# Squaring block 2's rows ahead of block 1's, its diagonal two stages earlier, and a fourth temporary buffer in phase three

## The chip, the cores and the metric

The kernel runs on one core of a Trainium2 chip. Its time is the device time of one execution in microseconds (us), the median of several; a profile is one execution recorded by the hardware profiler, with times counted from its first instruction. The engines are TensorE (PE, with its weight loads PEld), VectorE (DVE), ScalarE (ACT) and GpSimd (POOL). SyncE (SP) issues most loads, POOL issues the stores of the first part; each queue issues in order, and an instruction that waits holds back everything behind it on its queue.

## The reference

One step of a decoder layer on 4096 prompt tokens and 64 sample tokens (8 sequences of 8), with a model width of 1024, in float32:

```
def _layer(x, ...):
    h = _rmsnorm(x, g_pre)            # x * rsqrt(mean(x*x) + eps) * g_pre, row by row
    z = h @ w_in                      # 1024 -> 2816 columns
    ... gated short convolution, sliding-window attention, attention to 256 memory tokens ...
    y = concatenate([out_a, out_b, out_c]) @ w_out
    return x + _rmsnorm(y, g_post), ...
```

The change touches the first two lines only: how the factor rsqrt(mean(x*x) + eps) of each token, its row factor, comes to the place where the product h @ w_in is formed. It also touches the temporary tiles in which parts of z are kept until they are stored. What is computed stays the same.

## The kernel before

**Blocks, phases, steps.** The 4160 tokens are cut into 8 blocks (b = 0 to 7) of 520. A block's x stands transposed, in four operands B11, B21, B12, B22: the first digit is the half of the 1024 inputs, the second the half of the 520 tokens (128 partitions x 4 x 260 each). The 22 column tiles of w_in are taken in three phases (`PHASES`, L44) of 8, 8 and 6 tiles. "Phase three" is index 2. Within a phase each block is seven products of sums of weight quarters with sums of operands (`PRODUCTS`, L41; T1 to T4 are differences of the B operands, formed by `t_sum`), so that seven steps do the work of eight. Each product is three matmuls with operands split into a high and a low part (`split`, L357: `hi` by ScalarE, `lo` by VectorE, L360 and L361), all on L370.

**The plain blocks.** Blocks 0 and 1 of the first phase (`PLAIN_BLOCKS = 2`) run as eight plain products instead, the stages (b, s) with s = 0 to 7 of `PLAIN` (L578). TensorE can start on them before any row factor is known: the factors are multiplied into the results z afterwards (`z_rows`, L621). From block 2 on the operands are scaled before the product: `gain` (L326, ScalarE, by g_pre) and `scale` (L335, VectorE, by the row factors).

**Row factors.** For each block five groups of 104 tokens are loaded in natural layout (`row_load`, L255, on SP's queue), squared and summed by ScalarE (`row_step`, L269, L278), and turned into factors by POOL (L284, L285). j counts the groups, five to a block. From there two ways lead to a tile that has the 520 factors in every partition:
- For blocks 0 and 2 (`PLAIN_BLOCKS` is 2) `rows_diag` (L294) has VectorE write the factors on five diagonals, and `rows_product` (L302) has TensorE multiply them by ones; ScalarE copies the result out of PSUM (L308). `rows_bank` (L299) takes the PSUM bank for it.
- For the other blocks POOL stores the 520 factors to memory (`rowd`, L290, an issue of its own for 2 KB with the elements apart), and SP loads them back, broadcast to all partitions (`rows_load`, L251, L253). The load is issued a number of stages after the store: `row_spreads[b] = 4` counts down once a stage in `row_queue` (L310). Block 0 is stored too, for the next phase.

**The order of the work.** In the plain blocks and all of the first phase the order on every engine's queue is that of the program, by hand (`manual_schedule`, L697). `plain_loads` (L660) gives the loads of a stage, x operands first and then `row_queue`; `plain_jobs` (L628) gives a list of jobs for each stage, and `plain_block` (L674) spreads that list over the four quarters of the stage's matmuls, in proportion. With s at 2, 3, 6, 7 the second and the fourth quarter are followed by copies of the accumulators out of PSUM (L688). A natural row tile j >= 14 is loaded a stage after a square has freed its place (`row_loads`).

In the kernel before, the squares of block 1 (j = 5 to 9) end in stage (0, 7), and its store of factors follows there; those of block 2 (j = 10 to 14) end in (1, 2). The diagonal of block 2 is written in (1, 4) and multiplied in (1, 5). Block 1's factors are loaded in (1, 3) and first used by `z_rows(1, 1)` in (1, 7). Block 2's operands are loaded in (1, 2) to (1, 5), in the order B11, B21, B12, B22. Their gains and scales are jobs of (1, 4) to (1, 7).

**Phase three.** Phases two and three are ordered by the program's own scheduler, but for single instructions that are kept in place. `temp` (L170) hands out the temporary tiles. In phase three there are two pools of three tiles, `t2a` and `t2b` (L118), taken in turn unless the caller names one; each call turns the turn. `finish_parts` (L401) takes two for a tile of z in block 0: `zh`, the high part (L411), from pool a for the first row of a pair and from b for the second, and `kl_`, the low part (L413), by the turn. Later blocks write the low part in place. Both parts are stored to memory by SP (`qd`, L168), and a tile can be taken again when its store has landed.

Of the kernel before, what the change touches and what calls it, by code (L numbers as in the profile page):

```python
# [12 lines left out]
ALU = mybir.AluOpType  # L13
# [7 lines left out]
NS = 64  # L21
# [23 lines left out]
PLAIN_BLOCKS = 2  # L45
# [7 lines left out]
def hybrid_layer(ctx: ExitStack, tc: tile.TileContext, a: dict):  # L53
    nc = tc.nc
    TE, V, S, G, DMA = nc.tensor, nc.vector, nc.scalar, nc.gpsimd, nc.sync
# [40 lines left out]
    own = ExitStack()  # L96
# [6 lines left out]
    def open_phase(ph):  # L103
        nonlocal tp, natp, pa2, pa1, wide
        wide = 0 if ph == 0 else 2

        if ph == 0:
            z = [z_pool(kept_z, f"z{n}") for n in range(4)]
            natp = own.enter_context(tc.tile_pool(name="nat", bufs=2))
            zp[2] = [*z, z_pool(own, "z4")]  # L110
            kept_z.z4 = zp[2][-1]
        elif ph == 1:
            zp[2].remove(kept_z.z4)
            zp[2][:0] = [z_pool(own, f"z{n}") for n in (5, 6, 7)]
# [129 lines left out]
    RG = 104  # L244
# [3 lines left out]

    row_loads, row_spreads = [], {}

    def rows_load(b, again=False):  # L251
        rows[b] = (temp(f"rb{b}")[:, : 2 * HW] if again else natp.tile([P, 2 * HW], F32, tag="rb", name=f"rb{b}"))
        DMA.dma_start(rows[b], rowd[b].partition_broadcast(P))  # L253

    def row_load(j):  # L255
        if j < 5 * NBLK:
            g = RG * j - NS
            if 2 <= j < 10 or 12 <= j < 14:
                t = (wa if j < 7 or j == 12 else wb).tile([P, 2, 512], F32, tag="w", name=f"nat{j}")
                t = nat[j] = t.rearrange("p a n -> p (a n)")  # L260
            else:
                t = nat[j] = natp.tile([P, D], F32, tag="nat", name=f"nat{j}")
            if g < 0:
                DMA.dma_start(t[:NS], a["x_s"])
                DMA.dma_start(t[NS:RG], a["x_p"][: RG - NS, :])
            else:
                DMA.dma_start(t[:RG], a["x_p"][g : g + RG, :])

    def row_step():  # L269

        j = sq[0]
        if j == 5 * NBLK:
            return
        b, i = divmod(j, 5)
        if i == 0:
            nat["r"] = tiny.tile([P, 8], F32, tag="r", name=f"r{b}", bufs=3)
        r, t = nat["r"], nat.pop(j)
        S.activation(t[:RG], t[:RG], AF.Square, accum_out=r[:RG, i : i + 1])  # L278
        if j in (10, 11) or j >= 14:
            row_loads.append(after_nat[0])  # L280
            after_nat[0] += 1
        sq[0] += 1
        if i == 4:
            G.tensor_scalar(r[:RG, 0:5], r[:RG, 0:5], 1.0 / D, EPS, op0=ALU.mult, op1=ALU.add)  # L284
            G.tensor_tensor(r[:RG, 0:5], r[:RG, 0:5], mhalf[:RG, 0:5], op=ALU.pow)  # L285
# [4 lines left out]
            G.dma_start(rowd[b].rearrange("(i p) -> p i", p=RG), r[:RG, 0:5])  # L290
            if b > 0:
                row_spreads[b] = 4

    def rows_diag():  # L294

        for i in range(5):
            V.tensor_scalar(diag[:RG, RG * i : RG * (i + 1)], ident[:RG, :RG], nat["factors"][:RG, i : i + 1], None, op0=ALU.mult)

    def rows_bank(b):  # L299
        rows[b] = accumulator(1, 2, f"rows_y{b}")[:, :, :HW]  # L300
# [327 lines left out]
    def plain_jobs(b, s):  # L628

        gains = lambda b, *os: [lambda o=o: x_gain(0, b, o) for o in os]  # L630
        scales = lambda b, *os: [lambda o=o: x_scale(0, b, o) for o in os]
        parts = lambda b, o: [lambda: x_split(b, o)]
        fill = lambda o: [lambda q=q: first_fill(o, q) for q in range(4)]
        sums = lambda q, k: [lambda: first_sums(q, k)]
        fills = lambda q, *os: [lambda o=o: first_fills(q, o) for o in os]
        done = lambda b, row: finish(0, b, zz[b], row)
        row = [row_step]
        return {
            (0, 0): lambda: [*fill("A11"), *parts(0, "B21")],
            (0, 1): lambda: fill("A22"),  # L640
            (0, 2): lambda: [*fill("A12"), *parts(0, "B12"), *row],
            (0, 3): lambda: [*sums(0, 0), *row, *sums(0, 1), *fills(0, "S2"), *row],
            (0, 4): lambda: [*parts(0, "B22"), *fills(0, "S3", "S1"), *row, *fills(0, "S4"), *row],
            (0, 5): lambda: [*sums(1, 0), *row, *sums(1, 1), *fills(1, "S2", "S3"), *row],
            (0, 6): lambda: [*parts(1, "B11"), *row, *fills(1, "S1", "S4"), *sums(3, 0), *row],
            (0, 7): lambda: [*row, *fills(3, "S2", "S3"), lambda: rows_diag()],
            (1, 0): lambda: [*parts(1, "B21"), *row, *row, lambda: rows_bank(0), lambda: rows_product(0), *z_rows(0, 1)],
            (1, 1): lambda: [*z_rows(0, 0), *done(0, 1), *row, *row],
            (1, 2): lambda: [*parts(1, "B12"), *done(0, 0), *fills(3, "S1"), *row],
            (1, 3): lambda: sums(2, 0),  # L650
            (1, 4): lambda: [*row, lambda: rows_diag(), lambda: rows_bank(2), *parts(1, "B22"), *gains(2, "B11"), *sums(2, 1),
                             *fills(2, "S2")],
            (1, 5): lambda: [lambda: rows_product(2), *fills(2, "S3"), *row, *fills(2, "S1"), *gains(2, "B21"), *fills(2, "S4"),
                             *row],
            (1, 6): lambda: [*scales(2, "B11"), *gains(2, "B12"), *scales(2, "B21", "B12"), *row],
            (1, 7): lambda: [lambda: h_split(0), *gains(2, "B22"), *scales(2, "B22"), lambda: t_sum(0, 2, "T1"), *row,
                             *z_rows(1, 1)],
        }[b, s]()
# [1597 lines left out]
```

## Time and profile before

| | |
|---|---|
| median of three runs | 1470.48 us (1470.12 to 1474.75) |
| the profiled execution's own time | 1470.74 us |
| its span, first to last instruction | 1469.0 us |
| granted TensorE clock, mean | 0.999 |
| busy: PE, DVE, ACT, POOL | 1453.3, 1235.0, 888.9, 431.9 us |
| the plain blocks, stage (0, 0) to (1, 7) | about 6 to 100 us |
| phase three | about 662 to 930 us |

A line of a timeline gives start and duration in us, the engine, the line of the kernel, the operation with the tile that it writes and those that it reads, the shape, how many instructions are merged, and in brackets how long the engine was idle before it and what ended that. `SPq` and `ACTq` are an engine's issuing side. Names of tiles stand without their numbers at the end, so `hi_1B` is any high part of block 1's B operands. A line of waits gives the waiting engine, tile and line, what it waited for, the total in us, how often, and the longest. Matmul durations are modelled and overlap; their starts tell more.

### The profile page before, as it was taken

How to read it: one execution, taken by the hardware profiler on the slowest of the kernel's cores; microseconds unless marked ns; L12 is line 12 of the kernel's file. 1: busy time of each engine (PE TensorE's matmuls, PEld its weight loads, DVE VectorE, ACT ScalarE, POOL GpSimd, SP SyncE). 2: the span in 40 equal slices, each digit the busy share in tenths (PEclk: the TensorE clock that was granted, in tenths of full speed). 3: DMA queues.
4: the chain of work that ended last, by engine and by line, in shares of the span. 5: the costliest groups of instructions: out<-in, count | busy, mean ns of one | idle time of the engine just before them, and what ended most of it. 6: DMA issues, size and time to landing. Idle time of an engine off the chain costs nothing.

```text
span 1469.0 us, 31997 instructions
## 1 busy us (share of the span) xinstructions
PE 1453.3 (99%) x11887; PEld 1342.3 (91%) x11887; DVE 1235.0 (84%) x1991; ACT 888.9 (61%) x2170; POOL 431.9 (29%) x544
## 2 busy tenths in 40 slices
PE   9999999999999999999999999999999999999997
PEld 9999999999999999999999999778888888888875
DVE  6779887899988888798677777899998999999975
ACT  6776565566532222244545444788888878888862
POOL 0222322312403474300021130234334333433452
PEclk9999999999999999999999999999999999999999
DMA  9999999887866676688897679997887788888876
GB/s 265 191 248 223 297 275 265 248 288 248 216 229 244 243 248 232 225 284 253 281 233 266 215 215 329 279 280 240 252 263 241 240 243 268 243 248 264 254 266 224
DMA packets 233744, 369.59 MB, mean 252 GB/s; under 512 B 38501, under 2 KB 144485, under 8 KB 233557
## 3 DMA queue, kind: packets, MB, share of 16 engines
q1 hardware_dynamic: 210549, 314.66, 69.4%
q0 software_dynamic: 22320, 51.84, 12.4%
q8 instruction: 94, 1.54, 0.5%
q10 hardware_dynamic: 720, 1.05, 0.2%
q14 instruction: 61, 0.50, 0.1%
HBM read 251.00 MB, written 117.46 MB: 251 GB/s over the span
## 4 chain that ended last, share of the span: by engine, by line
PE 89%; DVE 4%; DMA 3%; ACT 2%; issue 1%; POOL 0%; ACTq 0%; SPq 0%; DVEq 0%; POOLq 0%
PE c L370 54%; PE y_c L1701 20%; PE ws L1394 3%; PE wo L1508 2%; PE wo L1115 2%; PE xs L1441 2%; PE wo L1503 1%; PE wt L1461 1%; PE xt L1461 1%; PE mem_acc L797 1%; DMA md<-th 1%; DMA nat<-in_x_p 1%; DMA ws4A<-in_w_in 1%; PE y L2069 1%; DMA md<-cacc 0%
## 5 line engine op out<-in xcount | busy, mean ns | idle before, releaser
L377 DVE TENSOR_TENSOR z<-c,z 128x520 f32<-128x520 f32 (+1 forms) x308 | 193.8, 643 | 71.8 <-PE c L370 70.8
L1425 ACT ACTIVATE sm<-sm,wnm 128x129 f32<-128x129 f32 x240 | 93.5, 392 | 13.8 <-DVE wrd L1429 7.1
L1701 PE MATMUL y_c<-wob,rows 128*128 128x512 f32 x384 | 95.8, 396 | 0.4 <-ACT s L1739 0.4
L1701 PE MATMUL y_c<-woT,a 128*128 128x512 f32 x384 | 95.2, 395 | 0.0
L1701 PE MATMUL y_c<-woT,down 128*128 128x512 f32 (+1 forms) x396 | 95.2, 389 | 0.0
L1701 PEld LDWEIGHTS y_c<-wob,rows 128*128 128x128 f32 x384 | 70.6, 188 | 17.5 <-ACT wpt L1366 2.4
L1701 PEld LDWEIGHTS y_c<-woT,down 128*128 128x128 f32 x396 | 71.7, 188 | 15.8 <-DVE swnm L1996 0.4
L1701 PEld LDWEIGHTS y_c<-woT,a 128*128 128x128 f32 x384 | 70.6, 188 | 15.2
L1232 ACT ACTIVATE xp<-xs,xnm 128x256 f32<-128x256 f32 x128 | 59.9, 483 | 20.4 <-PE wo L1115 13.5
L918 POOL TENSOR_TENSOR os0T<-os0T,os1T 128x512 f32<-128x512 f32 x20 | 29.0, 1448 | 125.2 <-DMA os1T<-in_w_out 75.8
L411 ACT CAST zh<-z 128x520 fp32r<-128x520 f32 x56 | 33.3, 625 | 40.9 <-DVE z L377 32.9
L1394 PEld LDWEIGHTS ws<-ring,q 128*128 128x128 f32 (+1 forms) x480 | 48.6, 186 | 8.4 <-issue 1.2
L278 ACT ACTIVATE nat<-nat 104x1024 f32<-104x1024 f32 x40 | 42.3, 1057 | 23.0 <-DMA nat<-in_x_p 23.0
L1411 DVE COPY_PREDICATED sm<-wmask,ws 128x512 f32<-128x512 uint8 x60 | 43.7, 754 | 14.6 <-ACT sm L1405 14.6
L1455 ACT ACTIVATE xp<-xp,xrd 128x256 f32<-128x256 f32 x120 | 53.9, 503 | 2.1 <-DVE xrd L1238 1.1
L1394 PE MATMUL ws<-ring,q 128*128 128x256 f32 (+1 forms) x480 | 54.0, 294 | 1.1 <-issue 0.6
L1366 ACT COPY wpt<-wt 128x512 f32<-128x512 f32 x60 | 33.9, 593 | 27.4 <-PE wo L1508 27.4
L379 ACT COPY z<-c 128x520 f32<-128x520 f32 (+1 forms) x44 | 24.2, 553 | 43.0 <-PE c L370 40.0
L1701 PE MATMUL y_c<-woT,diag 128*128 128x512 f32 x192 | 48.8, 400 | 0.0
L1369 POOL TENSOR_SCALAR_AFFINE_SELECT wpt<-wpt 128x512 f32<-128x512 f32 x64 | 46.1, 740 | 7.0 <-ACT wpt L1368 6.9
L1641 POOL TENSOR_TENSOR yst<-yst,mhalf 128x1 f32<-128x1 f32 (+1 forms) x33 | 20.4, 617 | 93.7 <-DVE yst L1640 93.7
L166 POOL DMA_DIRECT2D md<-th x48 | 26.2, 547 | 67.6 <-DVE th L430 59.4
(1055 smaller groups left out, 5537.9 us busy)
## 6 DMA issues: line engine op xcount, KB each, us to landing
woT<-tdT SPq DMA_DIRECT2D x75, 512.0 KB
q<-qd SPq DMA_DIRECT2D x112, 192.0 KB
xr<-in_x_p SPq DMA_DIRECT2D x32, 512.0 KB
nat<-in_x_p SPq DMA_DIRECT2D x39, 416.0 KB
o_yp<-xr SPq DMA_DIRECT2D x31, 512.0 KB
md<-th POOLq DMA_DIRECT2D x48, 260.0 KB, 7.2
qd<-zh SPq DMA_DIRECT2D x48, 260.0 KB
qd<-z SPq DMA_DIRECT2D x42, 260.0 KB
```

Of the source, the lines that this page charges most:

```text
L278: S.activation(t[:RG], t[:RG], AF.Square, accum_out=r[:RG, i : i + 1])
L370: TE.matmul(bank[:, :HW], l, r, start=first and i == 0, stop=last and i == 3 * KH - 1)
L377: add = lambda dst, other: V.tensor_tensor(dst, c, other, op=ALU.add)
L411: S.copy(hi, z)
L1232: S.activation(p[:, i, :], s[:, i, :], AF.Exp, bias=nm[:, i : i + 1], scale=SCALE, accum_out=den[:, i : i + 1])
L1366: S.copy(p3.rearrange("p h (r q) -> p r h q", r=2), t)
L1369: select = lambda out, step, op, slope: lambda: G.affine_select(out, p3, pattern=[[0, 4], [step, P]], compare_op=op, fill=0.0, base=0, cha ...
L1394: TE.matmul(out(kvh, col, bank), q(kvh, col, bank)[r], k(kvh, part)[r], start=first, stop=True, skip_group_check=not first, **place)
L1411: V.copy_predicated(self.of[i].sms[kvh][:, :, :P].rearrange("p (h a) k -> p a h k", a=2), third["wmask"].unsqueeze(1).to_broadcast([P, 2, ...
L1425: S.activation(sm[:, hh, :], sm[:, hh, :], AF.Exp, bias=nm[:, hh : hh + 1], scale=SCALE, accum_out=den[:, hh : hh + 1])
L1455: S.mul(p[:, i, :], p[:, i, :], self.rds[h][:, i : i + 1])
L1701: TE.matmul(self.acc[bank], self.parts[name][:, l, j], wo[o][j][:, r, cs], start=new and j + i == 0, stop=j == 3 and i == 2, skip_group_ch ...
```

## The change

Three edits. First, rows are squared in another order: `row_block` exchanges blocks 1 and 2, so that j = 5 to 9 are block 2's groups and j = 10 to 14 block 1's. The loads (`row_load`), the accumulators and the factors follow. Block 1's factors are therefore stored in (1, 2) instead of (0, 7), and their load comes two counts after the store instead of four, in (1, 4). The factors of blocks 0 and 2 are kept apart by key. Second, block 2's diagonal is written at the end of (1, 2) instead of in (1, 4); its product stays in (1, 5). The job list of (1, 2) grows from seven to eight, that of (1, 4) shrinks by one, and the spread over the quarters follows. Third, pool `t2b` of phase three gets a fourth tile.

```
-            tp = [own.enter_context(tc.tile_pool(name=f"t2{n}", bufs=3)) for n in "ab"]
+            tp = [own.enter_context(tc.tile_pool(name=f"t2{n}", bufs=3 + (n == "b"))) for n in "ab"]
...
+    def row_block(n):
+        return {1: 2, 2: 1}.get(n, n)
...
-            g = RG * j - NS
+            g = RG * (5 * row_block(j // 5) + j % 5) - NS
...
-        b, i = divmod(j, 5)
+        b, i = row_block(j // 5), j % 5
...
             if b in (0, PLAIN_BLOCKS):
-                nat["factors"] = r
+                nat["factors", b] = r
             if b == PLAIN_BLOCKS:
                 return
             G.dma_start(rowd[b].rearrange("(i p) -> p i", p=RG), r[:RG, 0:5])
             if b > 0:
-                row_spreads[b] = 4
+                row_spreads[b] = 2 if b < PLAIN_BLOCKS else 4
...
-            (1, 2): lambda: [*parts(1, "B12"), *done(0, 0), *fills(3, "S1"), *row],
+            (1, 2): lambda: [*parts(1, "B12"), *done(0, 0), *fills(3, "S1"), *row, lambda: rows_diag(2)],
             (1, 3): lambda: sums(2, 0),
-            (1, 4): lambda: [*row, lambda: rows_diag(), lambda: rows_bank(2), *parts(1, "B22"), *gains(2, "B11"), *sums(2, 1),
+            (1, 4): lambda: [*row, lambda: rows_bank(2), *parts(1, "B22"), *gains(2, "B11"), *sums(2, 1),
                              *fills(2, "S2")],
```

`rows_diag` takes the block as its argument; the call for block 0 in (0, 7) is otherwise unchanged.

More of the change, by code (lines that the diff above doesn't have):

```diff
@@ L291, in row_step, with rows_diag @@
             if b > 0:
-                row_spreads[b] = 4
-    def rows_diag():
+                row_spreads[b] = 2 if b < PLAIN_BLOCKS else 4
+    def rows_diag(b):
         for i in range(5):
-            V.tensor_scalar(diag[:RG, RG * i : RG * (i + 1)], ident[:RG, :RG], nat["factors"][:RG, i : i + 1], None, op0=ALU.mult)
+            V.tensor_scalar(diag[:RG, RG * i : RG * (i + 1)], ident[:RG, :RG], nat["factors", b][:RG, i : i + 1], None, op0=ALU.mult)
     def rows_bank(b):
@@ L645, in plain_jobs @@
             (0, 6): lambda: [*parts(1, "B11"), *row, *fills(1, "S1", "S4"), *sums(3, 0), *row],
-            (0, 7): lambda: [*row, *fills(3, "S2", "S3"), lambda: rows_diag()],
+            (0, 7): lambda: [*row, *fills(3, "S2", "S3"), lambda: rows_diag(0)],
             (1, 0): lambda: [*parts(1, "B21"), *row, *row, lambda: rows_bank(0), lambda: rows_product(0), *z_rows(0, 1)],
             (1, 1): lambda: [*z_rows(0, 0), *done(0, 1), *row, *row],
-            (1, 2): lambda: [*parts(1, "B12"), *done(0, 0), *fills(3, "S1"), *row],
+            (1, 2): lambda: [*parts(1, "B12"), *done(0, 0), *fills(3, "S1"), *row, lambda: rows_diag(2)],
             (1, 3): lambda: sums(2, 0),
-            (1, 4): lambda: [*row, lambda: rows_diag(), lambda: rows_bank(2), *parts(1, "B22"), *gains(2, "B11"), *sums(2, 1),
+            (1, 4): lambda: [*row, lambda: rows_bank(2), *parts(1, "B22"), *gains(2, "B11"), *sums(2, 1),
                              *fills(2, "S2")],
```

## The prediction

> **What bounds the kernel now.** I read the page first, then the stretches by engine, then TensorE's waits, and last the timelines around the two waits that lie where the change works.
>
> ```profile
> PE 1453.3 (99%) x11887; PEld 1342.3 (91%) x11887; DVE 1235.0 (84%) x1991; ACT 888.9 (61%) x2170; POOL 431.9 (29%) x544
> ...
> 0.00:115.00 115.00, 113.18 (x914) 112.11 (x915) 83.37 (x134) 83.36 (x162) 21.95 (x38) 1.00 0.94 227
> 656.00:930.00 274.00, 272.75 (x2228) 266.08 (x2226) 204.61 (x330) 130.21 (x238) 31.31 (x47) 1.00 0.80 250
> ```
>
> The columns of a stretch are its length, the busy time of PE, PEld, DVE, ACT and POOL, the granted clock, the DMA share and GB/s. TensorE is busy 99% of the span, so an edit elsewhere is worth only what it takes from TensorE's waits, or adds to them. The plain blocks and the first steps after them (0 to 115 us) leave TensorE idle 115.00 - 113.18 = 1.8 us; phase three (656 to 930 us) leaves 1.25 us. That is the most the change can win in its two places: 3 us, or 0.2%. Its possible loss has no such cap.
>
> ```profile
> PE c L370 <- DVE lo_1B L361: 1.0, 1, 1.0
> PE c L370 <- DVE lo_2T L361: 0.2, 1, 0.2
> ...
> 111.74 0.28 PE L370 MATMUL c<-hi_2T,w_0S 128*128 128x260 f32 x1
> 112.21 0.39 PE L370 MATMUL c<-lo_2T,w_0S 128*128 128x260 f32 x1 [0.18 <-DVE lo_2T L361]
> ...
> 696.24 0.28 PE L370 MATMUL c<-hi_1B,w_2A 128*128 128x260 f32 x1
> 696.36 0.28 PE L370 MATMUL c<-hi_1B,w_0A 128*128 128x260 f32 x1
> 697.60 0.39 PE L370 MATMUL c<-lo_1B,w_0A 128*128 128x260 f32 x1 [0.96 <-DVE lo_1B L361]
> ```
>
> Two waits of TensorE on L370 matter. Matmuls start 0.12 us apart when nothing holds them (696.24 to 696.36), so the first wait costs 112.21 - 111.74 - 0.12 = 0.35 us and the second 697.60 - 696.36 - 0.12 = 1.12 us.
>
> **The fourth buffer of pool t2b.** In phase three `temp` takes pools a and b in turn. Counting its calls, b receives two weight tiles of the first step, then the three `kl_` tiles of block 0's first row, then the second row's zh, kl_, zh, kl_, zh, kl_. With three buffers the second row's first zh follows the first kl_ (9004), and its first kl_ (9072) follows the second (9021):
>
> ```profile
> 689.27 0.32 SPq L168 DMA_DIRECT2D qd<-kl__9004  x1
> 690.18 0.81 SPq L168 DMA_DIRECT2D qd<-kl__9021  x1
> 694.28 0.63 ACT L411 CAST zh<-z 128x520 fp32r<-128x520 f32 x1 [3.75 <-DMA qd<-kl__9004]
> 694.81 1.05 ACT L360 CAST hi_1B<-x_1B 128x1040 fp32r<-128x1040 f32 x1
> 695.69 0.70 DVE L413 TENSOR_TENSOR kl__9072<-z,zh 128x520 fp32r<-128x520 f32 x1 [2.85 <-DMA qd<-kl__9021]
> 696.31 1.24 DVE L361 TENSOR_TENSOR lo_1B<-x_1B,hi_1B 128x1040 fp32r<-128x1040 f32 x1
> ```
>
> With four, that zh follows a weight tile that is long used up, and 9072 follows 9004, whose store has landed by 694.28 instead of 695.69. So 9072 runs 1.41 us earlier, and lo_1B ends near 697.55 - 1.41 = 696.14, before TensorE asks for it at 696.36 + 0.12. The wait of 1.12 us goes; what is late next is the same pair of tiles one step on, with some 4 us of matmuls ahead of it. The edit adds no instruction. Value: -1.1 us, between -1.25 (all idle of that stretch) and 0 (the program orders phase three itself, and with another buffer it may put the 9072 subtraction or the zh cast elsewhere).
>
> **The diagonal, two stages up.** Five multiplications leave VectorE's queue in stage (1, 4) and enter at the end of (1, 2):
>
> ```profile
> 81.86 1.00 DVE L297 TENSOR_SCALAR mix_s<-ident,r 104x104 f32<-104x104 f32 x5
> 84.72 0.59 ACT L308 COPY rb<-rows_y 128x520 f32<-128x520 f32 x1 [1.20 <-PE rows_y L306]
> ```
>
> They end 1.9 us before ScalarE may read the product, and the product itself stays in (1, 5), behind a quarter of that stage's matmuls. ScalarE waits for TensorE there, and not for the diagonal. Value 0; if the cover were gone, 1.0 us.
>
> **The order of the squares.** Ten squares, ten loads of the same sizes, one store of row factors and one load of them trade places: the counts stay, so the order itself costs 0. What moves is the pair store and load of block 1's factors (`rowd[1]`). The store goes from the end of (0, 7) to the end of (1, 2), past the md, zd and qd stores on POOL; the load goes from (1, 3) to (1, 4) on SP, past the two loads of block 2's B12. Between them lie two stages instead of four. How long does such a store take?
>
> ```profile
> 54.23 0.99 POOL L290 DMA_DIRECT2D rowd<-r  x1 [0.31 <-POOL r L285]
> DMA to landing us min/median/max: 9.3/11.8/14.5
> L253 SPq EVENT_SEMAPHORE  x6: 17/17/17, 78.2 to 266.7; - x6
> 54.00:61.00 7.00, 7.00 (x57) 6.88 (x56) 5.55 (x13) 5.69 (x13) 0.99 (x1) 1.00 0.90 209
> 61.00:67.00 6.00, 6.00 (x53) 6.00 (x52) 4.41 (x6) 2.52 (x5) 2.23 (x4) 1.00 1.18 79
> 67.00:75.00 8.00, 8.00 (x69) 8.00 (x69) 3.14 (x7) 4.95 (x10) 1.08 (x2) 1.00 0.99 285
> ```
>
> The second line is the answer for the tile rowd: its stores take 9.3 to 14.5 us to land. The third shows that the load L253 carries a wait on SP. The stretches show what the store does beside that: some 7 us after its issue, all transfers together fall to 79 GB/s for 6 us. TensorE stays full in it.
>
> The Trainium skill, page "DMA: Bandwidth & Descriptors", section "Latency and other measured facts", gives a DMA a fixed cost of about 2 us. By that the store would be down before SP asks, and the sum would be that of the second rival below, 1469.6 us. The row of landing times disagrees by a factor of five. The same page's "Rules for kernel authors" tells us to issue a DMA early and to wait for it late, and the edit does the reverse.
>
> *When the store starts.* In (1, 2) the last square releases it:
>
> ```profile
> 68.29 1.06 ACT L278 ACTIVATE nat<-nat 104x1024 f32<-104x1024 f32 x1 [4.77 <-DMA nat<-in_x_p]
> 74.20 0.64 ACT L429 ACTIVATE th<-z 128x520 f32<-128x520 f32 x1 [1.61 <-DMA md<-th]
> 76.61 1.07 ACT L278 ACTIVATE nat<-nat 104x1024 f32<-104x1024 f32 x1
> 78.36 1.19 POOL L285 TENSOR_TENSOR r<-r,mhalf 104x5 f32<-104x5 f32 x1
> ```
>
> At the old times it would start at 78.36 + 1.19 + 0.31 = 79.9 us. But the slow stretch at 61 to 67 us belongs to the store that is no longer there, and the square at 68.29 and the tanh at 74.20 wait for transfers out of it. Up to 4.77 us come back, so the start lies between 75.1 and 79.9. I take 76.0, nearer the early end, since both waits have the same cause.
>
> *When it lands.* Between 9.3 and 14.5 us later. Here SP, once held, adds no traffic of its own, so I take 10.5, between the shortest and the median 11.8: 86.5 us.
>
> *What stands behind it.* SP reaches the load of `rowd[1]` well before that and stops. Queued behind it are the two loads of block 2's B22 and the natural rows of the 17th square, which now leave late. ScalarE waits for those rows already:
>
> ```profile
> 78.23 0.34 SPq L253 DMA_DIRECT2D rb<-rowd  x1
> 82.19 10.73 SPq L267 DMA_DIRECT2D nat<-in_x_p  x3
> 91.43 1.06 ACT L278 ACTIVATE nat<-nat 104x1024 f32<-104x1024 f32 x1 [1.90 <-DMA nat<-in_x_p]
> 97.62 0.60 ACT L688 COPY z<-c 128x520 f32<-128x520 f32 x1 [0.26 <-PE c L370]
> 98.11 1.72 ACT L328 ACTIVATE place<-place,gpre 128x260 f32<-128x260 f32 x4
> 110.92 1.23 DVE L361 TENSOR_TENSOR lo_2T<-x_2T,hi_2T 128x1040 fp32r<-128x1040 f32 x1
> 99.90:112.10 12.20, 12.12 (x102) 11.91 (x100) 12.20 (x13) 8.24 (x15) 5.82 (x8) 1.00 0.86 200
> nat<-in_x_p SPq DMA_DIRECT2D x3, 416.0 KB
> rb<-rowd SPq DMA_DIRECT2D x1, 260.0 KB
> qd<-zh POOLq DMA_DIRECT2D x1, 260.0 KB, 3.5
> 83.00:91.00 8.00, 8.00 (x66) 7.88 (x66) 6.10 (x11) 5.33 (x12) 0.00 (x0) 1.00 0.95 235
> ```
>
> From 91.43 on ScalarE works in order, with one pause of 0.26 us, up to the gains of B22 at 98.11, and from their end VectorE is busy for all of 12.20 us until lo_2T, the tile of the first wait above. So whatever the 17th rows are late beyond 0.26 us reaches TensorE in full. Once the hold ends, 260 KB of factors, 520 KB of B22 (128 x 1040 x 4 bytes) and 416 KB of rows have to come: 1196 KB, which at 235 GB/s is 5.2 us. The lead is some 2 us: a lone 260 KB transfer lands in 3.5 us, of which about 1.1 us is its bytes. So 7 us, from 5.5 (the queue empty) to 9.2 (82.19 to 91.43, a full queue). The rows come at 86.5 + 7.0 = 93.5, which is 2.1 us after 91.43, and 1.8 us beyond the pause. Value +1.8 us. Bounds: 75.1 + 9.3 + 5.5 = 89.9 gives 0; 79.9 + 14.5 + 7.0 = 101.4 gives +9.7.
>
> **Sum.** -1.1 + 0 + 0 + 1.8 = +0.7 us. The profiled execution took 1470.74 us (span 1469.0, the rest around it); the median of the runs shown is 1470.48, 0.26 below. On the execution's own time: 1471.4 us.
>
> **The rivals.**
> - *The hold runs long (slower than before).* Nothing comes back from the old slow stretch, because the tanh at 74.20 has other stores ahead of it, and the store starts at 79.9 us and takes the median 11.8: it lands at 91.7, the rows come at 98.7, 7.0 us late beyond the pause. 1470.74 + 7.0 - 1.1 = 1476.6 us. It decides the sign from a landing after about 85.8 us, and passes 0.3% (4.4 us) from 90.2 us on. For it: every row of landing times is over 9 us. Against it: the 4.77 us wait has no other owner in the trace. Chance 0.16.
> - *The hold costs nothing.* The store starts early and lands before 84.7 us, or the loads behind it come in well under 7 us since the queue is empty. Then only the buffer counts: 1470.74 - 1.1 = 1469.6 us. For it: the shortest landing is 9.3 us, and SP, held, adds no traffic. Against it: it needs the early end of two terms at once. Chance 0.24.
> - *The buffer does not do what it is for.* Phase three is put in order by the program itself, which may place the casts so that lo_1B still ends late; the hold stays as forecast: 1470.74 + 1.8 = 1472.5 us. Chance 0.10.
>
> **How the numbers follow.** The forecast has the remaining 0.50, at 1471.4 us; its own range, with a hold worth 0.5 to 4 us, is 1470.1 to 1473.6. The low end of the range is the second rival with the 0.35 us of lo_2T won as well and the median's 0.26 below, 1469.0; the high end, 1476.0, is a hold of 6.4 us with the buffer's gain. Outside lie about 0.1 above and 0.06 below. A difference of 0.3%, 4.4 us, is about what a measurement of this kernel can tell from no change. Slower by more than that is most of the first rival: 0.14. Faster by more than that needs more than the 3 us of idle that the two places have: 0.03. The rest, 0.83, is within it.
>
> **What would show it.** In the changed profile SP's load L253 for block 1 should start at 84 to 90 us, with a gap before it that the store rowd ended, and the two B22 loads and the rows after it. ScalarE's 17th square should start about 93 us instead of 91.43, and TensorE's wait for lo_2T near 112 us should be 2 us instead of 0.35. VectorE's five multiplications should stand near 78 us, and the slow stretch near 78 to 84 us instead of 61 to 67. In phase three the wait for lo_1B near 697 us should be gone. If SP's load isn't held, or TensorE idles nowhere near 100 to 115 us, the hold is wrong; a wait of over 5 us there makes the first rival right.

## The result and the profile after

The changed kernel takes 1478.3 us (median of 7 runs, 1475.03 to 1481.49); the kernel before, timed beside it, took 1470.87 (7 runs, 1470.12 to 1474.75). The ratio is 1.0045, with a 95% interval of 1.0029 to 1.0061. Timed again later (e5 below) it took 1476.4 (5 runs), ratio 1.0035 (1.0023 to 1.0047). So the change makes the kernel slower, by 0.2 to 0.6%. The profiled execution of the changed kernel took 1475.97 us, with a span of 1474.3: 5.3 us more than the 1469.0 of before. It is the second fastest of the seven executions: the medians lie 7.4 us apart, and what the slower executions lose beyond the 5.3 us is in no profile kept here. Lines from L251 on have moved down by 4, so the matmul line L370 is now L374, and the square L278 is L282.

TensorE does the same work (11887 matmuls) and idles more in one place. Stretches of the changed kernel, with the same columns as before; the first three have the bounds of those shown of before:

```profile
PE 1455.1 (99%) x11887; PEld 1343.7 (91%) x11887; DVE 1232.3 (84%) x1991; ACT 889.0 (60%) x2170; POOL 433.1 (29%) x544
...
0.00:115.00 115.00, 109.70 (x871) 108.26 (x872) 77.98 (x128) 78.95 (x156) 22.20 (x35) 0.99 0.87 224
656.00:930.00 274.00, 273.69 (x2238) 267.25 (x2236) 205.39 (x329) 131.20 (x238) 31.36 (x47) 1.00 0.80 252
61.00:67.00 6.00, 6.00 (x53) 6.00 (x52) 6.00 (x9) 5.62 (x12) 1.27 (x3) 1.00 1.02 218
79.00:84.00 5.00, 5.00 (x43) 4.97 (x42) 4.06 (x8) 3.09 (x8) 0.98 (x1) 1.00 0.52 117
82.00:87.00 5.00, 5.00 (x41) 4.88 (x40) 1.78 (x3) 2.35 (x6) 0.00 (x0) 1.00 0.00 0
84.00:87.00 3.00, 3.00 (x25) 2.91 (x24) 0.69 (x1) 2.26 (x5) 0.00 (x0) 1.00 0.00 0
87.00:92.00 5.00, 5.00 (x44) 5.00 (x44) 3.12 (x4) 2.54 (x6) 0.04 (x1) 1.00 0.69 67
92.00:97.00 5.00, 5.00 (x45) 5.00 (x44) 0.57 (x1) 0.00 (x0) 1.06 (x2) 1.00 1.04 304
100.00:105.00 5.00, 1.56 (x9) 1.15 (x9) 2.48 (x2) 5.00 (x12) 0.53 (x1) 0.97 0.60 150
105.00:112.00 7.00, 7.00 (x49) 7.00 (x48) 6.88 (x6) 4.75 (x9) 3.88 (x4) 0.78 0.86 278
```

Up to 115 us the idle time grew from 1.8 to 5.3 us, and what is new of it lies at 100 to 105 us. In phase three it fell from 1.25 to 0.31. The slow transfers at 61 to 67 us are gone (79 GB/s before, 218 now). A hole of another kind stands from about 82 us on: nothing at all moves at 82 to 87 us, and then 67 GB/s until 92. The DMA share tells the two apart: at 61 to 67 us before it was 1.18, so the DMA engines were full and moved little; at 82 to 87 us it is 0.00, so they had nothing to do.

What happened is read on three queues. POOL's work on block 1's factors and its store, SP's queue, and ScalarE's and TensorE's timelines of the changed kernel:

```profile
75.72 1.25 POOL L288 TENSOR_SCALAR r<-r 104x5 f32<-104x5 f32 x1
77.05 1.64 POOL L289 TENSOR_TENSOR r<-r,mhalf 104x5 f32<-104x5 f32 x1
78.99 0.99 POOL L294 DMA_DIRECT2D rowd<-r  x1 [0.30 <-POOL r L289]
```
```profile
75.78 1.45 SPq L240 DMA_DIRECT2D place<-in_xt  x2
87.28 0.34 SPq L257 DMA_DIRECT2D rb<-rowd  x1
87.72 0.94 SPq L240 DMA_DIRECT2D place<-in_xt  x2
88.77 9.97 SPq L271 DMA_DIRECT2D nat<-in_x_p  x3
```
```profile
63.60 1.06 ACT L282 ACTIVATE nat<-nat 104x1024 f32<-104x1024 f32 x1
...
64.65 1.05 ACT L282 ACTIVATE nat<-nat 104x1024 f32<-104x1024 f32 x1
...
71.84 0.64 ACT L433 ACTIVATE th<-z 128x520 f32<-128x520 f32 x1 [2.59 <-DMA md<-th]
...
84.74 0.59 ACT L312 COPY rb<-rows_y 128x520 f32<-128x520 f32 x1 [2.65 <-PE rows_y L310]
...
97.25 1.06 ACT L282 ACTIVATE nat<-nat 104x1024 f32<-104x1024 f32 x1 [7.71 <-DMA nat<-in_x_p]
```
```profile
103.03 0.39 PE L374 MATMUL c<-hi_2B,w_0A 128*128 128x260 f32 x1 [2.55 <-ACT hi_2B L364]
104.30 0.39 PE L374 MATMUL c<-lo_2B,w_0A 128*128 128x260 f32 x1 [0.89 <-DVE lo_2B L365]
...
117.46 0.39 PE L374 MATMUL c<-lo_2T,w_0S 128*128 128x260 f32 x1
```

The store of block 1's factors is issued at 78.99 us. SP issues the two loads of B12 at 75.78 and then nothing, until the load of those factors goes out at 87.28. That is the moment at which the store has landed, 8.3 us after its issue. Behind the load come B22 and the natural rows; ScalarE's 17th square (j = 17) waits 7.71 us for its rows and starts at 97.25 instead of 91.43. TensorE then stands twice, for hi_2B and for lo_2B, and lo_2T enters at 117.46 instead of 112.21.

The copy of the diagonal's product (84.74, and 84.72 before) is a common mark ahead of the trouble. From it to the first matmul on lo_2T are 27.48 us before and 32.72 after: 5.24 us lost. From there to the end both executions need the same (1356.8 and 1356.7 us). So in this pair the whole 5.3 us of the span comes from this place. Executions differ behind it, though: over the 13 profiles of this document the way from lo_2T to the end takes 1354.5 to 1358.9 us, so a span alone doesn't tell what this place cost, and the 27.48 us do.

### The profile page after: what moved, and what is told of

It is laid out like the page before. It is cut to its first block, busy times and chain, and to the rows that moved or that the text cites. A ratio compares the mean times of both kernels' runs of the same rounds, so it can differ in the third digit from the quotient of the medians.

```text
span 1474.3 us, 31993 instructions
## 1 busy us (share of the span) xinstructions
PE 1455.1 (99%) x11887; PEld 1343.7 (91%) x11887; DVE 1232.3 (84%) x1991; ACT 889.0 (60%) x2170; POOL 433.1 (29%) x544
## 3 DMA queue, kind: packets, MB, share of 16 engines
q0 software_dynamic: 22320, 51.84, 12.4%
HBM read 251.00 MB, written 117.46 MB: 250 GB/s over the span
## 4 chain that ended last, share of the span: by engine, by line
PE 91%; DVE 3%; DMA 3%; ACT 2%; issue 1%; ACTq 0%; DVEq 0%
PE c L374 55%; PE y_c L1705 21%; PE ws L1398 3%; PE wo L1512 2%; PE wo L1119 2%; PE xs L1445 2%; DMA nat<-in_x_p 2%; PE wo L1507 1%; PE wt L1465 1%; PE xt L1465 1%; PE mem_acc L801 1%; PE y L2073 1%; DMA woT<-tdT 0%; DVE z L381 0%; DMA wr_1A<-in_w_in 0%
## 5 line engine op out<-in xcount | busy, mean ns | idle before, releaser
L1429 ACT ACTIVATE sm<-sm,wnm 128x129 f32<-128x129 f32 x240 | 93.5, 392 | 13.5 <-DVE wrd L1433 7.1
L1705 PEld LDWEIGHTS y_c<-wob,rows 128*128 128x128 f32 x384 | 70.6, 188 | 17.5 <-ACT wpt L1370 2.4
L922 POOL TENSOR_TENSOR os0T<-os0T,os1T 128x512 f32<-128x512 f32 x20 | 29.5, 1476 | 126.7 <-DMA os1T<-in_w_out 53.8
L282 ACT ACTIVATE nat<-nat 104x1024 f32<-104x1024 f32 x40 | 42.2, 1056 | 22.6 <-DMA nat<-in_x_p 22.6
```

The lines of the kernel that those rows point to most:

```text
L1429: S.activation(sm[:, hh, :], sm[:, hh, :], AF.Exp, bias=nm[:, hh : hh + 1], scale=SCALE, accum_out=den[:, hh : hh + 1])
L1705: TE.matmul(self.acc[bank], self.parts[name][:, l, j], wo[o][j][:, r, cs], start=new and j + i == 0, stop=j == 3 and i == 2, skip_group_ch ...
```

## The experiments

The theory after the result was that SP's held load costs the time: too short a way from store to load, with block 2's last operands and rows queued behind. Its rivals: the fourth buffer or another edit costs it; the slow transfers beside the store cost it, wherever the load stands; the half clock that follows TensorE's idle time makes it large. Every experiment is an edit of the changed kernel unless said otherwise. Each was timed against the kernel before on the same chip.

**The edits one by one.** The kernel before, with the fourth buffer alone:

```
+            tp = [own.enter_context(tc.tile_pool(name=f"t2{n}", bufs=3 + (n == "b"))) for n in "ab"]
```

> The kernel before with the fourth buffer of t2b alone. If the hold of SP's queue is the whole loss, this edit stands apart from it and is worth what phase three shows: TensorE's wait for lo_1B near 697 us (1.12 us) goes, some of it comes back at lo_1T a step later, where one subtraction of a kl_ tile has moved ahead: 0.6 to 1.1 us less than the kernel before. If the loss comes from phase three's new order, this run is slower than before by several us.

Measured: 1469.96 us, ratio 0.9997 (0.9988 to 1.0006). The wait of lo_1B is gone and its phase three (656 to 930 us) has TensorE busy for 273.44 us instead of 272.75. In the time, that can't be told from nothing.

The changed kernel with three buffers, as before:

```
+            tp = [own.enter_context(tc.tile_pool(name=f"t2{n}", bufs=3)) for n in "ab"]
```

> The changed kernel with three buffers in t2b again: the exchange of the squares and the moved diagonal alone. Hold theory: the whole loss and the lost millisecond share of the buffer, about 1 us slower than the changed kernel, SP held from about 77 to 87 us, TensorE idle near 100 to 104 us. Phase-three theory: close to the kernel before, 1471 us.

Measured: 1475.53 us, ratio 1.0033 (1.002 to 1.0045). The order of the rows and the diagonal alone carry the loss; the buffer is out of it. The 1 us more than the changed kernel that was expected without the buffer does not show (1476.4 and 1478.3 with it).

**The load one stage later.** Three counts between store and load instead of two:

```
-                row_spreads[b] = 2 if b < PLAIN_BLOCKS else 4
+                row_spreads[b] = 3 if b < PLAIN_BLOCKS else 4
```

> The changed kernel with block 1's factors loaded three stages after the store instead of two, so that SP issues block 2's B22 and the rows of the 17th square before it stops. Hold theory: the wait for the store now has only the rows of the 18th square behind it, ScalarE's 17th square starts near 91.5 us as before the change, TensorE is not idle near 100 us and its clock stays full: 1469.5 to 1471 us. Rival, the store itself: it still falls between 79 and 90 us and slows all transfers, so B22 and the rows, issued into the slow stretch, come late by 3 to 6 us all the same: 1474 to 1477 us.

Measured: 1470.38 us, ratio 1.0003 (0.9994 to 1.0011). SP's queue, ScalarE's square and two stretches of this kernel:

```profile
74.28 2.92 SPq L240 DMA_DIRECT2D place<-in_xt  x4
79.00 0.34 SPq L271 DMA_DIRECT2D nat<-in_x_p  x1
87.35 0.35 SPq L257 DMA_DIRECT2D rb<-rowd  x1
```
```profile
90.07 1.06 ACT L282 ACTIVATE nat<-nat 104x1024 f32<-104x1024 f32 x1
```
```profile
84.00:87.00 3.00, 3.00 (x24) 2.88 (x24) 0.49 (x1) 1.64 (x3) 0.00 (x0) 1.00 0.34 23
87.00:92.00 5.00, 5.00 (x45) 5.00 (x44) 2.70 (x5) 4.22 (x10) 0.00 (x0) 1.00 0.40 66
```

Here B22 (now in the x4) and the rows of the 17th square go out ahead of the factors. SP is held until 87.35 all the same, and little moves meanwhile (23 and 66 GB/s). How much of that is slowness and how much an empty queue, these stretches don't tell. But nothing that is needed soon stands behind the held load, and the square starts without a wait. So the hold is harmless if the right things are ahead of it.

**The same order without the wait.** The load stays in its place and reads other factors, those of block 0, stored long ago:

```
-        DMA.dma_start(rows[b], rowd[b].partition_broadcast(P))
+        DMA.dma_start(rows[b], rowd[0 if b == 1 and not again else b].partition_broadcast(P))
```

> The changed kernel, but the load of block 1's factors in the plain blocks reads block 0's, which were stored 37 us earlier (z of block 1 is scaled by the wrong factors). All transfers stay, at the same places of their queues; only the wait for the late store is gone. Hold theory: as with three stages, 1469.5 to 1471 us, and no idle of TensorE near 100 us. Rival, the store itself: 1474 to 1477 us, for the store is still issued near 79 us and the loads behind it are still on their way.

Measured: 1470.53 us, ratio 1.0001 (0.9992 to 1.001). The store, issued at 79.90, runs as in the changed kernel, only nobody waits for it, and the loss is gone. Since SP goes on issuing, this run shows what the store does to other transfers:

```profile
87.00:92.00 5.00, 5.00 (x44) 5.00 (x43) 2.70 (x4) 3.58 (x8) 0.00 (x0) 1.00 0.53 42
```
```profile
92.79 1.06 ACT L282 ACTIVATE nat<-nat 104x1024 f32<-104x1024 f32 x1 [2.21 <-DMA nat<-in_x_p]
```

They move at 42 GB/s while ScalarE waits 2.21 us for the rows of the 17th square. TensorE loses nothing by it, but only just: the table at the end of this section puts the square 0.26 us inside the limit.

**The changed kernel again**, for a second profile:

> The changed kernel itself, for its time and its profile beside the three that follow. Hold theory: 1474 to 1479 us, SP held to 86 to 88 us, and a clock below 0.998 wherever TensorE's idle time near 100 us is long; since the buffer saves some 0.6 us, not slower than the exchange of the squares alone (1475.5 us) by more than a run's spread.

Measured: 1476.4 us, ratio 1.0035 (1.0023 to 1.0047). The loss to lo_2T is 6.23 us in this execution. Its store is issued at 77.03, SP's load goes out at 86.74, and the square starts at 96.98.

**The load a stage earlier still.**

```
+                row_spreads[b] = 1 if b < PLAIN_BLOCKS else 4
```

> The changed kernel with block 1's factors loaded one stage after the store, in (1, 3), ahead of block 2's B12 too. Hold theory: the store lands at the same 86 to 88 us, but now 520 KB more stand behind it, so the rows of the 17th square come some 2 us later than in the changed kernel, and B12's gain can be late as well: 2 to 3 us slower than the changed kernel, 1477 to 1482 us. If the hold weren't the cause, no difference.

Measured: 1473.87 us, ratio 1.0025 (1.0014 to 1.0036). This expectation missed: the 2 to 3 us more than the changed kernel are not there. SP's queue:

```profile
72.78 0.34 SPq L271 DMA_DIRECT2D nat<-in_x_p  x1
83.55 0.34 SPq L257 DMA_DIRECT2D rb<-rowd  x1
```

SP is held from 73 us on, so the loads of B12 that ran beside the store now stand behind it. The store is issued at 76.37 and lands in 7.2 us, but from the landing to the square it takes 11.1 us instead of 10.0. From issue to square that makes 18.24 us, and it was 18.26 in the changed kernel: what the landing gains, the longer queue behind it loses. The square comes earlier in this profile because the store was issued earlier, and that lies ahead of what the edit moves. Whether the median of 1473.87 is a gain over the 1476.4 of e5 stays open, since the two intervals overlap.

**The store in larger pieces.** The store of 520 single elements of 4 bytes becomes 104 pieces of 20 bytes, for block 1 alone:

```
-            G.dma_start(rowd[b].rearrange("(i p) -> p i", p=RG), r[:RG, 0:5])
+            G.dma_start(rowd[b].rearrange("(p i) -> p i" if b == 1 else "(i p) -> p i", p=RG), r[:RG, 0:5])
```

> The changed kernel with block 1's store of factors in pieces of 20 bytes, one a partition, instead of 520 elements of 4 bytes (block 1's factors then stand in another order, so its z is scaled wrongly). If it is the elements apart that make the store slow, it lands in 3 to 5 us instead of 8 to 10, the transfers aren't slowed after it, SP is held to about 82 us, and the time is 1470 to 1472 us. Rival, a store from POOL takes 8 us or more of itself: landing and time as in the changed kernel.

Measured: 1470.08 us, ratio 0.9997 (0.9988 to 1.0005). The hold is still there, but the store, issued at 81.42, is down at 85.75, in 4.3 us instead of 8.3. Both halves of the delay shrink: from the issue of the store to the 17th square it takes 12.4 us, against 18.3 in the changed kernel.

**The clock.** 24 spare matmuls ahead of the first step of block 2, so that TensorE does not idle there:

```
+                if i == 0 and q == 0:
+                    for _ in range(24):
+                        TE.matmul(acc[:, 0, :HW], ws[0, 3, "A12"][:, 0, 0:P], h0[1, "B22"][0][:, 0], start=True, stop=True)
```

> The changed kernel with 24 spare matmuls (2.85 us, overwritten by the product that follows) ahead of the first step behind the plain blocks, where TensorE waited 2.7 us for hi_2B. If the half clock comes from that idle time, it is gone: clock 0.998 or more in most runs, and the slowest runs come down; the median falls by 0 to 2.5 us, since VectorE's chain still sets the end at lo_2T. If the half clock has another cause, clock and time stay as in the changed kernel.

Measured: 1479.04 us, ratio 1.0043 (1.0028 to 1.0058). The half clock near 105 us is gone from this profile:

```profile
105.00:112.00 7.00, 6.32 (x52) 5.96 (x50) 6.13 (x6) 5.82 (x12) 3.12 (x4) 1.00 0.82 247
```

The clock is 1.00 where it was 0.78, and the loss to lo_2T is 5.06 us, as in the changed kernel. In the changed kernel's profile TensorE's new idle time was 3.5 us of the 5.24, and most of the rest passed at half clock. Here, at full clock, TensorE comes earlier and waits at lo_2T again, 0.45 us. So the clock is not where the time goes in these two executions: VectorE's chain sets when lo_2T is ready. The clock is 0.998 or more in five of the six runs, as expected, but the median did not fall, and the slowest run still takes 1479.49 us.

**A store in order and in larger pieces.** To keep the gain of the packed store with the right factors, the natural rows are dealt out by fives (partition p takes rows 5p to 5p+4), for all blocks:

```
-            G.dma_start(rowd[b].rearrange("(i p) -> p i", p=RG), r[:RG, 0:5])
+            G.dma_start(rowd[b].rearrange("(p i) -> p i", p=RG), r[:RG, 0:5])
...
-            V.tensor_scalar(diag[:RG, RG * i : RG * (i + 1)], ident[:RG, :RG], nat["factors", b][:RG, i : i + 1], None, op0=ALU.mult)
+            V.tensor_scalar(diag[:RG].rearrange("q (p i) -> q i p", i=5)[:, i], ident[:RG, :RG], nat["factors", b][:RG, i : i + 1], None, op0=ALU.mult)
...
+            if s:
+                DMA.dma_start(t[:s], a["x_s"][i :: 5, :])
+            DMA.dma_start(t[s:RG], a["x_p"][g : g + 5 * (RG - s - 1) + 1 : 5, :])
```

> The changed kernel with the natural rows dealt out the other way: partition p holds rows 5p to 5p+4, so the store of the factors leaves in pieces of 20 bytes in the right order, the loads of the rows take every fifth row, and the diagonal is written at every fifth place. All of the work is kept. Hold theory: the store of block 1's factors lands 4 to 5 us after it starts, as in the packed run (4.3 us), with little slow stretch behind it; the 17th square starts no more than 8 us behind the mark, and the kernel takes 1469 to 1471 us, the time before within 0.1 %. Rival (the loss belongs to the order of the squares or the diagonal, and the packed run won by its wrong factors): 1474 to 1478 us. A cost of its own is possible: a diagonal written with a stride of 20 bytes, 0 to 0.3 us more for each on its engine.

Measured: 1478.41 us, ratio 1.0044 (1.0031 to 1.0058): missed in the time, though not in the place. From the mark to lo_2T it needs 27.47 us, no loss. But the mark itself comes at 91.62 us, 6.9 us late, since TensorE stood ahead of it. One line of its waits, and the stretch in which it ends:

```profile
PE rows_y L310 <- ACT hi_1B L593: 4.6, 1, 4.6
```
```profile
61.00:67.00 6.00, 4.71 (x23) 4.36 (x24) 4.55 (x12) 4.69 (x11) 0.00 (x0) 0.72 0.47 122
```

The wait is 4.6 of the 6.9 us. In the stretch in which it ends the mean clock is 0.72, and TensorE starts 23 matmuls where it had started 53 before. The 64 sample tokens are dealt over all five groups of block 0 by this edit, so block 0's rows take ten loads instead of six, and x operands queue behind them in the first 30 us. The last experiment, which leaves block 0 alone, has no such wait (e7, which deals nothing out, has one of 1.1 us). The diagonal at a stride, changed here too, was not tried by itself, so which part of the edit makes the wait is argued and not shown.

**B22 ahead of the factors.** The two loads of B22 are asked for in (1, 4), with B12:

```
-                      (1, 4): [(2, "B12")], (1, 5): [(2, "B22")]}.get((b, s), ()):
+                      (1, 4): [(2, "B12"), (2, "B22")]}.get((b, s), ()):
```

> The changed kernel with block 2's quadrant B22 asked for ahead of the factors, in the same stage as B12, so that only the fourth group of rows stands behind the held load. Hold theory: the rows wait for the landing as before, but 0.34 MB less comes ahead of them after it: the 17th square starts 7 to 9 us after the landing instead of 10, 1 to 2.5 us earlier than in the changed kernel, and the kernel takes 1473 to 1476 us. If the slow stretch behind the store sets the start whatever is queued, nothing changes: 1476 to 1478 us. If the wait for the landing were of no account and only the amount of data were, the time before: 1470 us.

Measured: 1474.15 us, ratio 1.0026 (1.0014 to 1.0037). SP and ScalarE:

```profile
75.13 3.44 SPq L240 DMA_DIRECT2D place<-in_xt  x4
89.07 0.35 SPq L257 DMA_DIRECT2D rb<-rowd  x1
```
```profile
96.95 1.06 ACT L282 ACTIVATE nat<-nat 104x1024 f32<-104x1024 f32 x1 [7.30 <-DMA nat<-in_x_p]
```

Behind the landing the rows need 7.9 us instead of 10.0, as expected. But the store, issued at 78.29, now lands in 10.8 us instead of 8.3, with B22 moving ahead of it and beside it. The square gains 0.3 us, where 1 to 2.5 were expected. Most of what is taken from behind the hold is paid ahead of it. The median is lower than that of the changed kernel; its profiled span, 1474.1, is not, so a gain is left open.

**One block dealt out.** Only block 1's rows are dealt out by fives, with all of the work kept and no load added:

```
+            b, i = row_block(j // 5), j % 5
+            step = 5 if b == 1 else 1
+            g = RG * 5 * b - NS + (i if b == 1 else RG * i)
...
+                DMA.dma_start(t[:RG], a["x_p"][g : g + step * (RG - 1) + 1 : step, :])
...
+            G.dma_start(rowd[b].rearrange("(p i) -> p i" if b == 1 else "(i p) -> p i", p=RG), r[:RG, 0:5])
```

> The changed kernel, all of its work kept, with only block 1's natural rows dealt out by fives (partition p holds rows 5p to 5p+4), so that this one store leaves in 20-byte pieces in the right order; blocks 0 and 2 to 8 load, store and write their diagonals as in the changed kernel, so no load is added in the first 30 us. Hold theory: store of block 1's factors lands 3.5 to 5 us after its start, 17th square no more than 8 us behind the mark, lo_2T no more than 0.3 us later to the mark than before; 1469 to 1471 us. If dealing out all of the rows lost its time in the second stage of block 1 because of the rows' order in itself and not because of the three loads added at the start, TensorE waits 3 us or more for hi_1B again near 58 us, and the time is 1475 to 1479 us.

Measured: 1469.6 us, ratio 0.9993 (0.9984 to 1.0001). POOL, SP, ScalarE, TensorE and two stretches:

```profile
79.17 0.65 POOL L296 DMA_DIRECT2D rowd<-r  x1 [0.30 <-POOL r L291]
```
```profile
82.62 0.34 SPq L257 DMA_DIRECT2D rb<-rowd  x1
```
```profile
90.72 1.06 ACT L284 ACTIVATE nat<-nat 104x1024 f32<-104x1024 f32 x1 [1.33 <-DMA nat<-in_x_p]
```
```profile
112.08 0.39 PE L376 MATMUL c<-lo_2T,w_0S 128*128 128x260 f32 x1 [0.19 <-DVE lo_2T L367]
```
```profile
84.00:87.00 3.00, 3.00 (x25) 2.94 (x24) 0.69 (x1) 2.41 (x5) 0.00 (x0) 1.00 0.94 197
87.00:92.00 5.00, 5.00 (x44) 5.00 (x43) 3.27 (x4) 3.67 (x9) 0.20 (x1) 1.00 0.69 211
```

The store is down 3.5 us after its issue, SP goes on at 82.62, so the transfers run at about 200 GB/s where the changed kernel had 0 and 67, and nothing is lost. It is the same wait in the same queue, with a store that is fast enough. Against the kernel before it is no measurable gain either: the interval ends at 1.0001.

**All profiles on one line.** The mark is the start of ScalarE's copy of the diagonal's product (near 85 us); x is the time from there to the start of the 17th square. lo_2T enters with TensorE's first matmul on it, and y is by how much that lies further behind the mark than the 27.48 us of before (differences taken ahead of rounding).

| kernel | mark | 17th square | lo_2T enters | x | y |
|---|---|---|---|---|---|
| before | 84.72 | 91.43 | 112.21 | 6.71 | 0.00 |
| e1, buffer alone | 85.38 | 90.66 | 112.86 | 5.28 | 0.00 |
| e9, all blocks dealt | 91.62 | 96.33 | 119.09 | 4.71 | -0.01 |
| e3, load a stage later | 85.36 | 90.07 | 112.85 | 4.71 | 0.01 |
| e11, one block dealt | 84.59 | 90.72 | 112.08 | 6.13 | 0.01 |
| e4, no wait | 85.78 | 92.79 | 113.27 | 7.01 | 0.01 |
| e7, packed store | 86.51 | 93.83 | 114.05 | 7.32 | 0.06 |
| e2, three buffers | 86.03 | 95.55 | 115.76 | 9.52 | 2.25 |
| e6, load earlier | 84.75 | 94.61 | 114.83 | 9.86 | 2.60 |
| e10, B22 first | 84.84 | 96.95 | 117.17 | 12.11 | 4.84 |
| e8, spare matmuls | 86.69 | 99.01 | 119.23 | 12.32 | 5.06 |
| after | 84.74 | 97.25 | 117.46 | 12.51 | 5.24 |
| e5, after again | 84.52 | 96.98 | 118.23 | 12.46 | 6.23 |

Up to x = 7.27 nothing is lost; from there y = x - 7.27, to 0.01 us, in every row but the last. That is the mechanism: rows that come later than 7.27 us after the mark delay TensorE one to one. (The 7.27 is read off these rows.) In the last row VectorE had lo_2T ready at 115.91 + 1.23 = 117.14, on the line, and TensorE came to it 1.09 us later without a wait in between.

## Why the prediction was wrong

It foresaw 1471.4 us with a range up to 1476.0, and 0.14 for slower by over 0.3%. The mechanism was right, in its place and its chain; the sizes were not.

- **The hold of SP's queue: right in kind, mis-sized.** The prediction gave it 1.8 us; it is 5.24 in the profiled execution, and 5.19 by the same line in e5, the second profile of the same kernel. Its terms:

| term | forecast | changed kernel | e5 |
|---|---|---|---|
| the store is issued | 76.0 | 78.99 | 77.03 |
| from there to the landing | 10.5 | 8.3 | 9.7 |
| from the landing to the 17th square | 7.0 | 10.0 | 10.2 |
| the 17th square | 93.5 | 97.25 | 96.98 |

  In the profiled execution the store is 3.0 late, from there the rows need 18.26 us and not 17.5 (+0.8), and the pause that swallows lateness is 7.27 - 6.71 = 0.56 and not 0.26 (-0.3): 1.8 + 3.0 + 0.8 - 0.3 = 5.3.
- **The step that failed is the time of the rows, 93.5 us: two of its three terms came out too early in both profiles.** What stands behind the load took 10.0 and 10.2 us from the landing to the square instead of 7.0, and the store was issued 3.0 and 1.0 us after 76.0. The landing took less than the 10.5 us given to it, by 2.2 and 0.8, and that luck hid a part of both.
- **What stands behind the load.** The 7.0 let 1196 KB move at 235 GB/s from the landing on; the stretch of 87 to 92 us shows 67 GB/s instead. With the store in 20-byte pieces (e7, e11) it took 8.1 us, so some 1.9 of the missing 3.0 us go with the single elements and 1.1 do not. With single elements stored and the rows behind the hold, issue of the store to square took 17.7 to 20.0 us in all six profiles (after, e2, e5, e6, e8, e10), whatever was put ahead or behind; with 20-byte pieces 12.4 and 11.6 (e7, e11).
- **When the store starts.** The prediction took 76.0, near the early end, "since both waits have the same cause". The square's wait of 4.77 us did go: the two squares now stand back to back at 63.60 and 64.65. The tanh's wait did not go in the profiled execution: at 71.84 it waits 2.59 us for a store of md, where it was 1.61. POOL's work on the factors is queued behind that tanh's own md store, and so began only 2.4 us earlier than before. In e5 that tanh does not wait for md, and POOL began 4.3 us earlier. But in both POOL then needed 2.9 us for its two steps (1.25 + 1.64), where the old profile had shown 1.4 (0.19, and the 1.19 that the prediction added):

```profile
78.08 0.19 POOL L284 TENSOR_SCALAR r<-r 104x5 f32<-104x5 f32 x1
```

  That is 1.5 us of the start in either execution. The same two steps for block 0 had taken 2.4 us in the old profile (0.71 at 51.48 and 1.65 behind it), so the 1.4 was a short case; why it was short is open.
- **The first rival.** It had the argument on the tanh's other stores, and its price, 1476.6, is close to what was measured. The price is right partly by luck: it gave the landing 11.8 us and the rest 7.0, and measured were 8.3 and 10.0.
- **TensorE's wait was looked for in the wrong tile.** It was to appear at lo_2T, as 2 us. It shows earlier, at hi_2B and lo_2B (2.55 and 0.89 us), since those too are made behind the late square on ScalarE. At lo_2T none is left, since TensorE came there late itself, after 3.41 us at half clock; the sum is what counts there.
- **The buffer: right about the wait, and not measurable.** lo_1B is gone from TensorE's waits. In the changed kernel lo_1T comes late instead, by 707.93 - 707.40 - 0.12 = 0.41 us:

```profile
707.40 0.28 PE L374 MATMUL c<-hi_1T,w_0S 128*128 128x260 f32 x1
707.93 0.39 PE L374 MATMUL c<-lo_1T,w_0S 128*128 128x260 f32 x1 [0.24 <-DVE lo_1T L365]
```

  So phase three gained 1.25 - 0.31 = 0.94 us of the 1.1 forecast. It did not show in the span: other waits (lo_6B, 0.9 us, in phase two) came in this execution, and in none of the others did they; their cause is open. With three buffers in the new order (e2) TensorE waited only 0.2 us for lo_1B, so even the wait to be won isn't the same in every execution. In the times, 0.9997 (0.9988 to 1.0006) allows for the 1.1 us and for nothing.
- **The diagonal: right, worth 0.** It is written at 74.70 us (the prediction looked for it near 78), and ScalarE waits for TensorE's product, now 2.65 us instead of 1.20.
- **The squares' order by itself: right, worth 0.** With the wait taken out (e4), later (e3) or shortened (e11), the changed order costs nothing measurable.
- **The rule on issuing early.** The Trainium skill, page "DMA: Bandwidth & Descriptors", section "Rules for kernel authors", tells authors to wait late for a DMA issued early; the runs agree, by 1470.38 against 1476 to 1478 us for one stage more. The same section says that a strided last dimension becomes one descriptor per element and should be made contiguous. e7 and e11 agree: 4.3 and 3.5 us instead of 8.3. The second rule was on that page beside the first, and it bears on the row of landing times that the prediction quoted without asking why they are so long.

## What to carry to other kernels

A load that waits for a store holds everything queued behind it on its queue: before moving the two closer, list what stands behind the load and when it is needed, and put that ahead of it. When a wait in the old profile is expected to vanish, check each link between it and the instruction that you move: here the square was freed, and in one execution of two the store, queued behind another, was not. Make a small store that someone waits for leave in runs and not in single elements: here it landed in 3.5 to 4.3 us instead of 7.2 to 10.8, and what stood behind it came sooner too.

## What was not expected of the hardware

- Of the landing of a store of 520 single elements of 4 bytes, 2 KB in all, most is silence. In the changed kernel the core's DMA engines stand still from 82 us to the landing at 87.28, in e10 from 84 us to the landing at 89.07:

```profile
84.00:89.00 5.00, 5.00 (x41) 4.91 (x40) 1.38 (x2) 4.16 (x9) 0.00 (x0) 1.00 0.00 0
```

  SP is held and nothing else has been asked for, so whatever the store had to move had left by then, and its end was told 5 us later. With 104 pieces of 20 bytes (e11) the other transfers and the store are through by 82 us, and SP goes on at 82.62.
- While such a store has not landed, and shortly after, other transfers are slow. The 0 GB/s of the changed kernel does not show that, since there was nothing to move. The kernel before shows it, with 79 GB/s at a DMA share of 1.18 (61 to 67 us; landing 14.5 us after the issue at 54.23), and e4 with 42 GB/s while the square waits for its rows. The 67 GB/s of the changed kernel at 87 to 92 us come behind the landing. Why they are slow was not tried.
- The landing of such a store depends on what is asked for ahead of it: 7.2 us with SP held early (e6), 8.3 to 9.7 in four profiles with B12 ahead (after, e2, e5, e8), 10.0 and 10.8 with B12 and B22 (e3, e10).
- The granted clock can halve after a short idle time, for whole windows. In the changed kernel:

```profile
101.31:104.72 3.41, 0.81 (x4) 0.61 (x5) 1.70 (x2) 3.41 (x8) 0.53 (x1) 1.00 0.54 101
104.72:108.13 3.41, 3.41 (x18) 3.41 (x18) 3.01 (x3) 2.84 (x5) 1.31 (x3) 0.50 0.75 233
```

  A window of 3.41 us in which TensorE was busy for 0.81 is followed by one at 0.50. The Trainium skill, page "TensorE: Matmul & The Clock Gate", section "Part 1: The HAM clock gate", gives free-running windows of 3413 ns, and the length agrees; it asks for an idle window, and here one busy for a quarter of its time was enough. It does not always come: in e10 TensorE waits 2.1 and 0.9 us in the same place, and the clock stays at 1.00. In the changed kernel's profile the half clock cost nothing, as e8 shows. In e5 it lasts two windows (103.10 to 109.93 us), and that execution alone lies off the line of the table, by 1.04 us, with TensorE late and lo_2T ready; that the clock is the reason is argued and was not tried.
